# A decoder trunk in split fp32: when ScalarE copies the running sum of the feed-forward into its PSUM banks

## The chip, the cores and the metric

The kernel runs on one core of one Trainium2 chip. The metric is the device time of one execution in microseconds (us). Each kernel is run several times; before the change the median of three runs is 2176.53 us (2175.78 to 2177.68). One further execution was recorded by the profiler: 2176.25 us in all, of which 2174.5 us lie between its first and its last instruction (its span).

Engines, as the profile names them: PE is TensorE's matmul, PEld its weight load, DVE is VectorE, ACT is ScalarE, POOL is GpSimd, SP is SyncE, which issues nearly all DMAs here. A q behind a name means the engine's sequencer.

## The reference

Two decoder layers over 256 tokens of width 2048, in float32: a gated linear attention layer, then a differential attention layer, each followed by a feed-forward (FFN). What the change touches is the FFN alone:

```
def swiglu(h, w_gate_up, w_down):
    gate, up = jnp.split(h @ w_gate_up, 2, axis=-1)
    return (jax.nn.silu(gate) * up) @ w_down

for i in range(DEPTH):                       # DEPTH = 2
    ...                                      # mixer, x = x + rmsnorm(mix)
    f = swiglu(rmsnorm(x, pre_ffn_g[i]), ffn_w_gate_up[i], ffn_w_down[i])
    x = x + rmsnorm(f, post_ffn_g[i])
```

The hidden width is 5632, so `gate` and `up` have 11 chunks of 512 columns each, and the output has 4 chunks of 512.

## The kernel before

**Split products.** A float32 matmul is made of three products of a faster format: each operand is split into a high part (ScalarE's cast, L306) and a low part (VectorE subtracts the high part from the value, L309), and TensorE adds up high times high, high times low and low times high (L419 to L421, or L559 to L561). Weights come in blocks of 128 x 1024 (256 rows of a chunk of 512 columns). Each block is loaded by SP into one of five `raw` buffers, cast, subtracted, and lies then in one of nine places of a ring (`hi`, `lo`) until TensorE has used it.

**The weight stream.** The order in which blocks are needed is written out by hand (`weight_stream`, L84). `take` (L387) hands out the next block and calls `pump` (L380), which writes down conversions ahead of need, up to nine blocks past the last one freed, and loads up to five blocks past the last one converted.

**Who sets the order.** The program is traced from top to bottom, and a planner then simulates the engines and writes the order of each engine's instructions: of those that are ready in its simulation the one traced earlier goes first (`urgent` puts a piece ahead). On the chip each engine goes through its own order, so an instruction that waits holds up those behind it. `issue_after(x)` (used by `past`, L760, and `behind`, L395) forces what is traced inside it to come behind `x` on `x`'s engine.

**Up steps (duos).** For chunk c, `gated_duo` (L1253) makes gate and up together by `duo_seeded` (L490). Eight blocks of each of the two chunks are worked through, s = 0 to 7; the ones in `fast` (0, 2, 3, 4, 5, 6, or 0, 2, 4, 6 for c = 1) are combined by sums of blocks (kinds a to d, four conversions, L343 to L359), the others are done plainly; of a plain s below 7 the second chunk's block is kept for the end. The duo uses PSUM banks 0, 1, 3, 4, 5, 7 of the pool `acc` (six banks) and 2 and 6 of the pool `tp` (two). Behind the last fast step stands `early` (L1267): ScalarE copies bank 0 out (L1270), and VectorE takes differences with banks 5, 6 and 4 (L1259), one of which is the start value of bank 7. After it come the kept blocks, block 7 of the first chunk (banks 1 and 3) and block 7 of the second (banks 2 and 7), with `late` (L1276) behind each finished bank: sums on VectorE and the Silu on ScalarE (L1281).

**Down runs.** `down_act` (L462) multiplies the hidden chunks of one group (`FF_GROUPS`, L39: pairs of chunks, chunk 8 alone) with the down weights and adds to output chunks, two banks each (one for each half of the tokens). Only the first group starts from nothing. For all others the running sum, which lies in SBUF (`f_ffn`), is first copied into the two banks by ScalarE (L472), and TensorE adds onto it; at the end the banks are copied back (L1335). Down runs and duos alternate (`ffn_steps`, L60). In each FFN nine down runs begin with such copies: eight directly behind a duo, the ninth behind another down run.

In the text d0 and d1 are the first and second block of a down run, and blocks 7 the last ones of a duo. The functions that the change touches:

Of the kernel before, what the change touches and what calls it, by code (L numbers as in the profile page):

```python
# [54 lines left out]
def ffn_pairs(c):  # L55

    return FAST_SECOND if c == 1 else FAST_FFN
# [139 lines left out]
class Trunk:  # L197
    def __init__(self, ctx, tc, t):
        self.ctx, self.tc, self.nc, self.t = ctx, tc, tc.nc, t

        def pool(name, **kw):
            return ctx.enter_context(tc.tile_pool(name=name, bufs=1, **kw))

        self.const = pool("const")
        self.big = pool("big")
        self.ring = pool("ring")
        self.hs = pool("hs")
        self.psum = pool("psum", space=bass.MemoryType.PSUM)
        self.dram = pool("dram", space=bass.MemoryType.DRAM)
        self.n = 0  # L210
        self.later = []
        self.stream = weight_stream()
        self.loads = load_list(self.stream)
        self.n_used = self.n_done = 0
        self.subs = {}
        self.split_off = None
        self.parts = {}
        self.raws = {}
        self.n_dma = self.n_conv = self.n_take = self.n_free = 0
        self.pool_lo = set()  # L220
        self.n_narrow = 0
        self.cap = 2
        self.ident = self.const.tile([P, P], F32, tag="ident", name="ident")
# [78 lines left out]
    def split(self, src, gp=False):  # L302
        nc = self.nc
        w = src.shape[-1]
        hi, lo = self.places(w)
        cast = nc.scalar.copy(hi, src)  # L306
        eng = nc.gpsimd if gp else nc.vector
        with self.past(self.split_off):
            rest = eng.tensor_tensor(out=lo, in0=src, in1=hi.bitcast(F32), op=ALU.subtract)  # L309
        if not gp:  # L310
            self.parts[self.n_conv] = cast.ins, rest.ins
        return hi, lo
# [66 lines left out]

    def pump(self):  # L380
        n = len(self.stream)
        while self.n_conv < min(n, self.n_free + NRING, self.n_take + self.cap):
            self.convert()
            while self.n_dma < min(len(self.loads), self.n_done + NRAW):
                self.load()
# [76 lines left out]
    def down_act(self, aT, w, s0, order, ns, evac, skew=0, base=None):  # L462

        ps, taken = {}, {}

        def run(u, b):
            c, s = order[u]
            if c not in ps:
                ps[c] = [self.acc(), self.acc()]
                if base:  # L470
                    for i in range(2):
                        self.nc.scalar.copy(ps[c][i], base(c, i))  # L472
            if not b:
                taken[u] = self.take(w, (c, s0 + s))
            self.mm_act(ps[c][b], aT, b, s, taken[u], ns, base is not None)
            if s == ns - 1:
                evac(c, b, ps[c][b])
            if b:
                self.free()
            self.tick()  # L480

        n = len(order) - skew
        for u in range(n):
            run(u, 0)
            run(u, 1)
        for b in range(2):
            for u in range(n, len(order)):
                run(u, b)

    def duo_seeded(self, aT, forms, fast, chunks, early, late):  # L490

        ps, held = {}, []
        (w1, n1), (w2, n2) = chunks

        def bank_of(bank):
            if bank not in ps:
                ps[bank] = self.tp().rearrange("p j t -> p (j t)") if bank in (2, 6) else self.acc()
                return True
            return False

        def add(bank, a, wp, j, last, onto=False):
            first = bank_of(bank)
            self.triple(ps[bank], a, wp, j, first and not onto, last, onto)

        def plain(bank, s, b, wp, last, onto=False):
            for j in range(2):
                add(bank, aT.tokens(2 * s + j, b), wp, j, last and j == 1, onto)
            if last:
                with self.behind(LATE_BEHIND):
                    late(bank, ps)  # L510
            self.tick()

        for s in range(7):
            k1, k2 = 2 * s, 2 * s + 1
            if s not in fast:
                wp = self.take(w1, (n1, s))
                for b, bank in enumerate((1, 3)):
                    plain(bank, s, b, wp, False)
                self.free()
                held.append(s)  # L520
                continue
            f, last = forms.pairs.index(s), s == fast[-1]
            plan = {
                "a": ((0, aT.tokens(k1, 0)), (1, aT.tokens(k2, 0))),
                "b": ((6, forms.fast(f, 2)), (2, forms.fast(f, 3))),
                "c": ((5, forms.fast(f, 1)), (3, aT.tokens(k2, 1))),
                "d": ((4, forms.fast(f, 0)),),
            }
            for kind, prods in plan.items():
                wp = self.take("duo", (*chunks, s), kind)  # L530
                for j, (bank, a) in enumerate(prods):
                    add(bank, a, wp, j, last and bank in (0, 4, 5, 6))
                self.free()
                if kind != "d":
                    self.tick()
            if last:
                bank_of(7)
                with self.behind(EARLY_BEHIND):
                    self.urgent(early)(ps)
        kept = [(s, self.take(w2, (n2, s))) for s in held]  # L540
        for s, wp in kept:
            plain(2, s, 0, wp, False)
        wp = self.take(w1, (n1, 7))
        for b, bank in enumerate((1, 3)):
            plain(bank, 7, b, wp, True)
        for s, wp2 in kept:
            plain(7, s, 1, wp2, False, True)
            self.free()
        self.free()
        wp = self.take(w2, (n2, 7))  # L550
        plain(2, 7, 0, wp, True)
        plain(7, 7, 1, wp, True, True)
        self.free()
# [696 lines left out]
        self.defer(5, lambda: next_gain(3))  # L1250
        self.chunk_act(aT, w, 3, 8, self.urgent(evac(3)), tail=SKEW)

    def gated_duo(self, hT, forms, w, c, rs, new_sg):  # L1253

        nc = self.nc
        made = []

        def op(out, in0, in1, how):
            nc.vector.tensor_tensor(out=out, in0=in0, in1=in1, op=how)  # L1259

        def gated(b, up):
            sg = made[0]
            nc.vector.scalar_tensor_tensor(
                out=sg[:, b, :], in0=up, scalar=rs[b], in1=sg[:, b, :], op0=ALU.mult, op1=ALU.mult
            )

        def early(ps):  # L1267
            made.extend((new_sg(), self.scratch()))
            sg, v = made
            nc.scalar.copy(sg[:, 0, :], ps[0])  # L1270
            op(v, ps[5], sg[:, 0, :], ALU.subtract)
            op(sg[:, 1, :], ps[6], v, ALU.subtract)
            op(ps[7], ps[4], sg[:, 1, :], ALU.subtract)
            op(v, ps[4], v, ALU.add)

        def late(bank, ps):  # L1276
            sg, v = made
            if bank in (1, 3):
                b = bank // 2
                op(sg[:, b, :], ps[bank], sg[:, b, :], ALU.add)  # L1280
                nc.scalar.activation(sg[:, b, :], sg[:, b, :], AF.Silu, scale=rs[b])  # L1281
            elif bank == 2:
                op(v, ps[bank], v, ALU.add)
                gated(0, v)
            else:
                gated(1, ps[bank])

        self.duo_seeded(hT, forms, ffn_pairs(c), ((w, c), (w, 11 + c)), early, late)
        return made[0]

    def ffn(self, fp, hT, rs, gi, wgu, wd, post, after, name, reload, side=None):
# [50 lines left out]
        def part(c, b):  # L1342
            return f[0][:, b, c * C : (c + 1) * C]

        f = []
        plan = ffn_steps()
        for n, (kind, which, *chunks) in enumerate(plan):
            if kind == "up":
                sg = self.gated_duo(hT, forms, wgu, which, rs, new_sg) if which else gated_first()
                follow = plan[n + 1]  # L1350
                wait = 4 if which else 1
                if follow[0] == "down" and which not in follow[1]:
                    wait = 2 * len(down_order(*follow[1:])) + 1
                self.defer(wait, lambda sg=sg, c=which: gate_T(sg, c))
                continue
# [17 lines left out]
                    with self.behind(DOWN_BEHIND):  # L1373
                        evac(grp, c, b, ps)

            base = None if which == first else part
            self.down_act(gTs[which], wd, 2 * which[0], down_order(which, chunks), 2 * len(which), done, skew, base)

    def values(self, vp, aT, rs, i, steps, every):
# [349 lines left out]
```

## Time and profile before

| | before |
|---|---|
| median of three runs | 2176.53 us |
| the profiled execution, whole | 2176.25 us |
| its span | 2174.5 us |
| TensorE busy (matmul) | 2153.9 us, 99% |
| VectorE busy | 1942.6 us, 89% |
| ScalarE busy | 1376.5 us, 63% |
| HBM, mean rate over the span | 202 GB/s |
| granted TensorE clock | 0.999 |

How to read what is quoted further down. A row of the timeline has the start in us from the span's beginning, the duration in us, engine, line, operation, the tiles written and read (out<-in), their shapes, how many instructions the row merges, and in brackets how long the engine sat idle before it and what ended that. A row of the waits has who waited for what, the total in us, how many times and the longest. Matmuls overlap: a new one starts every 0.23 us while each row shows 0.39, so a busy TensorE can still lose time between starts.

### The profile page before, as it was taken

Reading aid. Unit: us, or ns where it says so; the run is one execution under the profiler, and the core shown is the slowest. Engines: PE = TensorE matmul, PEld = TensorE weight load, DVE = VectorE, ACT = ScalarE, POOL = GpSimd, SP = SyncE. Lnnn points to the kernel's source line nnn. Section 1 sums busy time; section 2 is a strip of 40 time slices with the busy share of each in tenths; the row PEclk is TensorE's granted clock in tenths of the full one; section 3 lists DMA queues with packets and bytes.
Section 4 is the critical chain, followed back from the end, with each engine's and each line's share of the span. In section 5 each row is a group of like instructions: output and inputs, shape, how many; then the busy total and the mean of one; then the engine's idle time right before and its main releaser. Section 6 shows DMA issues by size and latency. Waiting matters only on the chain.

```text
span 2174.5 us, 28418 instructions
## 1 busy us (share of the span) xinstructions
PE 2153.9 (99%) x10044; PEld 1785.0 (82%) x10044; DVE 1942.6 (89%) x2666; ACT 1376.5 (63%) x1926; POOL 38.4 (2%) x66
## 2 busy tenths in 40 slices
PE   9999999999999999999999999999999999999998
PEld 7888788888888888888878888888888888888876
DVE  7989988999999999999798567889999999999996
ACT  8756655666666666666776455566656666666664
POOL 1000000000000000000000000000000000000000
PEclk9999999999999999999999999999999999999999
DMA  8545566566555666656767555465655556566664
GB/s 309 166 150 192 176 225 214 208 220 231 174 191 205 213 213 209 207 181 214 249 203 244 188 172 163 149 235 186 228 202 185 188 200 209 202 210 205 210 215 154
DMA packets 125043, 440.08 MB, mean 202 GB/s; under 512 B 14091, under 2 KB 16820, under 8 KB 123620
## 3 DMA queue, kind: packets, MB, share of 16 engines
q1 hardware_dynamic: 123724, 436.44, 59.3%
q10 hardware_dynamic: 1176, 1.84, 0.2%
q8 instruction: 78, 1.28, 0.2%
q14 instruction: 65, 0.53, 0.1%
HBM read 429.82 MB, written 9.97 MB: 202 GB/s over the span
## 4 chain that ended last, share of the span: by engine, by line
PE 88%; DVE 5%; DMA 3%; ACT 2%; issue 1%; SPq 0%; POOL 0%; ACTq 0%; DVEq 0%; POOLq 0%
PE acc L419 11%; PE acc L421 11%; PE acc L420 11%; PE acc L560 10%; PE acc L561 10%; PE acc L559 10%; PE acc L707 8%; PE acc L708 4%; PE tp L561 3%; PE tp L560 3%; PE tp L559 3%; DMA raw<-in_w_d_dram 2%; DVE lo L309 2%; ACT hi L306 2%; DVE raw L341 1%
## 5 line engine op out<-in xcount | busy, mean ns | idle before, releaser
L309 DVE TENSOR_TENSOR lo<-raw,hi 128x1024 fp32r<-128x1024 f32 x921 | 1098.4, 1218 | 131.3 <-ACT hi L306 125.8
L306 ACT CAST hi<-raw 128x1024 fp32r<-128x1024 f32 x923 | 946.9, 1051 | 376.5 <-PE acc L707 89.6
L419 PE MATMUL acc<-hi,f_ffn_gT 128*128 128x512 f32 x704 | 270.5, 392 | 6.1 <-ACT acc L472 6.0
L420 PE MATMUL acc<-lo,f_ffn_gT 128*128 128x512 f32 x704 | 272.6, 389 | 0.0
L421 PE MATMUL acc<-hi,f_ffn_gT 128*128 128x512 f32 x704 | 270.5, 389 | 0.0
L560 PE MATMUL acc<-lo,h_ffn 128*128 128x512 f32 x612 | 239.2, 391 | 0.1
L561 PE MATMUL acc<-hi,h_ffn 128*128 128x512 f32 x612 | 238.4, 390 | 0.0
L559 PE MATMUL acc<-hi,h_ffn 128*128 128x512 f32 x612 | 227.7, 389 | 0.0
L419 PEld LDWEIGHTS acc<-hi,f_ffn_gT 128*128 128x128 f32 x704 | 132.1, 188 | 38.6 <-ACT acc L472 11.1
L341 DVE TENSOR_TENSOR raw<-raw 128x512 f32<-128x512 f32 x232 | 159.2, 686 | 3.3
L421 PEld LDWEIGHTS acc<-hi,f_ffn_gT 128*128 128x128 f32 x704 | 132.2, 188 | 27.5
L420 PEld LDWEIGHTS acc<-lo,f_ffn_gT 128*128 128x128 f32 x704 | 132.2, 188 | 27.2
L560 PEld LDWEIGHTS acc<-lo,h_ffn 128*128 128x128 f32 x612 | 114.9, 188 | 26.2 <-DVE lo L309 1.0
L559 PEld LDWEIGHTS acc<-hi,h_ffn 128*128 128x128 f32 x612 | 114.9, 188 | 24.1
L561 PEld LDWEIGHTS acc<-hi,h_ffn 128*128 128x128 f32 x612 | 114.9, 188 | 23.1
L306 ACT CAST hi<-sum 128x512 fp32r<-128x512 f32 x72 | 44.8, 622 | 96.6 <-DVE sum L341 96.6
L306 ACT CAST f_ffn_rest<-sum 128x512 fp32r<-128x512 f32 x56 | 34.9, 623 | 95.6 <-DVE sum L341 95.6
L707 PE MATMUL acc<-h_q,hi 128*128 128x512 f32 x256 | 92.5, 401 | 0.0
L707 PE MATMUL acc<-h_kv,hi 128*128 128x512 f32 x256 | 90.7, 399 | 0.0
L707 PE MATMUL acc<-h_mix,hi 128*128 128x512 f32 x256 | 90.5, 398 | 0.0
L1335 ACT COPY f_ffn<-acc 128x512 f32<-128x512 f32 x80 | 46.7, 586 | 56.6 <-PE acc L421 56.1
L341 DVE TENSOR_TENSOR sum<-raw,raw 128x512 f32<-128x512 f32 x116 | 79.3, 683 | 0.1
(417 smaller groups left out, 4105.8 us busy)
## 6 DMA issues: line engine op xcount, KB each, us to landing
raw<-in_w_gu_dram SPq DMA_DIRECT2D x352, 512.0 KB, 4.4
raw<-in_w_d_dram SPq DMA_DIRECT2D x176, 512.0 KB, 4.5
raw<-in_gla_w_r_dram SPq DMA_DIRECT2D x32, 512.0 KB, 4.4
raw<-in_gla_w_v_dram SPq DMA_DIRECT2D x32, 512.0 KB, 4.0
raw<-in_gla_w_out_dram SPq DMA_DIRECT2D x32, 512.0 KB, 4.8
raw<-in_w_v_dram SPq DMA_DIRECT2D x32, 512.0 KB, 4.5
raw<-in_w_k_dram SPq DMA_DIRECT2D x32, 512.0 KB, 4.3
raw<-in_diff_w_q_dram SPq DMA_DIRECT2D x32, 512.0 KB, 3.5
```

The source lines that it names most:

```text
L306: cast = nc.scalar.copy(hi, src)
L309: rest = eng.tensor_tensor(out=lo, in0=src, in1=hi.bitcast(F32), op=ALU.subtract)
L341: return self.nc.vector.tensor_tensor(out=out, in0=in0, in1=in1, op=ALU.add)
L419: nc.tensor.matmul(ps, ah, rh, start=(kt == 0 and not onto), stop=False, skip_group_check=onto)
L420: nc.tensor.matmul(ps, ah, rl, start=False, stop=False, skip_group_check=onto)
L421: nc.tensor.matmul(ps, al, rh, start=False, stop=(kt == 2 * ns - 1), skip_group_check=onto)
L559: nc.tensor.matmul(ps, ah, wh, start=first, stop=False, skip_group_check=onto)
L560: nc.tensor.matmul(ps, ah, wl, start=False, stop=False, skip_group_check=onto)
L561: nc.tensor.matmul(ps, al, wh, start=False, stop=last, skip_group_check=onto)
L707: nc.tensor.matmul(ps, lh, aT.both(kt), start=(kt == 0), stop=False)
L708: nc.tensor.matmul(ps[:, SEQ:], ll, aT.hi(kt), start=False, stop=(kt == KT - 1))
L1335: nc.scalar.copy(fc, ps)
```

## The change

The copies into the first two banks of a down run that follows a duo are traced inside that duo instead of at the run's start: the first directly behind `early`, the second behind the sums of banks 1 and 3 (`ahead`). `self.led` holds the latest such copy until the down run begins; casts traced meanwhile are tied behind it on ScalarE. So that casts of down weights are not traced ahead of the first copy, `open_to` stops `pump` from the start of the last but one fast step until `early` is traced; the number of blocks it lets through is that of the rest of the duo (in the duo of chunk 1, which has further plain steps, two fewer). The limit holds in every duo; copies move only where the next step is a down run that adds to an existing sum. The copies of a run's second chunk, and both pairs of the run that follows another run, stay at the run.

```
@@ __init__
+        self.open_to = self.led = None
@@ split
-        cast = nc.scalar.copy(hi, src)
+        with self.past(self.led):
+            cast = nc.scalar.copy(hi, src)
@@ pump
-        while self.n_conv < min(n, self.n_free + NRING, self.n_take + self.cap):
+        while self.n_conv < min(n, self.n_free + NRING, self.n_take + self.cap, self.open_to or n):
@@ down_act, run
-                ps[c] = [self.acc(), self.acc()]
-                if base:
-                    for i in range(2):
-                        self.nc.scalar.copy(ps[c][i], base(c, i))
+                ps[c] = base(c) if base else [self.acc(), self.acc()]
+                self.led = None
@@ duo_seeded(self, aT, forms, fast, chunks, early, late, ahead)
+            if s == fast[-2]:
+                self.open_to = self.n_take + 8 + len(held) + 2
...
             if last:
                 bank_of(7)
                 with self.behind(EARLY_BEHIND):
                     self.urgent(early)(ps)
+                self.open_to = None
+                ahead(0)
...
         for b, bank in enumerate((1, 3)):
             plain(bank, 7, b, wp, True)
+        ahead(1)
@@ ffn
+        def seed(c, b):
+            ps = self.acc()
+            self.led = nc.scalar.copy(ps, part(c, b)).ins
+            return ps
+
         f = []
+        seeded = []
...
-                sg = self.gated_duo(hT, forms, wgu, which, rs, new_sg) if which else gated_first()
                 follow = plan[n + 1]
+
+                def ahead(b, follow=follow):
+                    self.led = None
+                    if follow[0] == "down" and f and follow[1] != first:
+                        seeded.append(seed(down_order(*follow[1:])[0][0], b))
+
+                sg = self.gated_duo(hT, forms, wgu, which, rs, new_sg, ahead) if which else gated_first()
+                self.led = None
...
-            base = None if which == first else part
+            base = None if which == first else lambda c: [seeded.pop(0) if seeded else seed(c, b) for b in range(2)]
```

More of the change, by code (lines that the diff above doesn't have):

```diff
@@ L488, in down_act, with duo_seeded @@
                 run(u, b)
-    def duo_seeded(self, aT, forms, fast, chunks, early, late):
+    def duo_seeded(self, aT, forms, fast, chunks, early, late, ahead):
         ps, held = {}, []
@@ L1251, in proj_out, with gated_duo @@
         self.chunk_act(aT, w, 3, 8, self.urgent(evac(3)), tail=SKEW)
-    def gated_duo(self, hT, forms, w, c, rs, new_sg):
+    def gated_duo(self, hT, forms, w, c, rs, new_sg, ahead):
         nc = self.nc
@@ L1286, in late @@
                 gated(1, ps[bank])
-        self.duo_seeded(hT, forms, ffn_pairs(c), ((w, c), (w, 11 + c)), early, late)
+        self.duo_seeded(hT, forms, ffn_pairs(c), ((w, c), (w, 11 + c)), early, late, ahead)
         return made[0]
```

## The prediction

> **What bounds the kernel now.** I read the page first, then who waits for whom, then three rows of the timeline around the start of one down run. The page gives the span and TensorE's share:
>
> ```profile
> span 2174.5 us, 28418 instructions
> PE   2153.9 (99%) x10044; PEld 1785.0 (82%) x10044; DVE 1942.6 (89%) x2666; ACT 1376.5 (63%) x1926; POOL 38.4 (2%) x66
> ```
>
> TensorE has work 99% of the time, so a change that takes no matmul away can win at most what TensorE still waits, about 20 us. Of the waits that the trace names, these two matter:
>
> ```profile
> PE acc L419 <- ACT acc L472: 6.0, 9, 1.4
> ...
> ACT hi L306 <- DMA raw<-in_w_d_dram: 60.0, 85, 3.0
> ```
>
> The first (waits of TensorE: us in total, times, longest) is the first product of a down run that waits for ScalarE's copy of the running sum. The second says that ScalarE stands before casts whose down weights have not landed. One start of a down run shows how the two belong together. ScalarE:
>
> ```profile
> 713.42 0.58 ACT L1270 COPY sg<-acc 128x512 f32<-128x512 f32 x1
> 713.90 2.00 ACT L306 CAST hi<-raw 128x1024 fp32r<-128x1024 f32 x2
> 716.27 1.05 ACT L306 CAST hi<-raw 128x1024 fp32r<-128x1024 f32 x1 [0.37 <-DMA raw<-in_w_d_dram]
> 718.39 1.06 ACT L306 CAST hi<-raw 128x1024 fp32r<-128x1024 f32 x1 [1.07 <-DMA raw<-in_w_d_dram]
> 719.35 1.10 ACT L472 COPY acc<-f_ffn 128x512 f32<-128x512 f32 x2
> ```
>
> The copy out of bank 0 (the duo's early step) comes first, then the casts of the duo's two last blocks (block 7 of either chunk), then the casts of the first two down blocks, d0 and d1, each behind a DMA, and only then the two copies, with no idle time ahead of them: they were ready and stood in ScalarE's order behind d1's cast, 1.07 us of which was a wait for data that the first product doesn't need. TensorE meanwhile:
>
> ```profile
> 717.21 0.40 PE L560 MATMUL acc<-lo,h_ffn 128*128 128x512 f32 x1
> ...
> 719.05 0.39 PE L560 MATMUL acc<-lo,h_ffn 128*128 128x512 f32 x1
> 719.28 0.39 PE L561 MATMUL acc<-hi,h_ffn 128*128 128x512 f32 x1
> 719.99 0.50 PE L419 MATMUL acc<-hi,f_ffn_gT 128*128 128x512 f32 x1 [0.33 <-ACT acc L472]
> 720.33 0.40 PE L560 MATMUL tp<-lo,h_ffn 128*128 128x512 f32 x1
> ...
> 721.71 0.39 PE L420 MATMUL acc<-lo,f_ffn_gT 128*128 128x512 f32 x1
> ```
>
> Matmuls follow each other every 0.23 us (719.05 to 719.28). The down run's first one, put ahead of the duo's last ones in TensorE's order, starts 0.71 after its predecessor: the wait costs 0.48, not 0.33, and the next spacing (0.34) 0.11 more. **Each listed wait costs its own length and 0.26 us.** The other eight:
>
> ```profile
> 844.96 0.50 PE L419 MATMUL acc<-hi,f_ffn_gT 128*128 128x512 f32 x1 [0.38 <-ACT acc L472]
> 908.68 0.50 PE L419 MATMUL acc<-hi,f_ffn_gT 128*128 128x512 f32 x1 [1.31 <-ACT acc L472]
> 1035.03 0.50 PE L419 MATMUL acc<-hi,f_ffn_gT 128*128 128x512 f32 x1 [1.44 <-ACT acc L472]
> 1677.66 0.50 PE L419 MATMUL acc<-hi,f_ffn_gT 128*128 128x512 f32 x1 [0.38 <-ACT acc L472]
> 1803.03 0.50 PE L419 MATMUL acc<-hi,f_ffn_gT 128*128 128x512 f32 x1 [0.45 <-ACT acc L472]
> 1928.32 0.50 PE L419 MATMUL acc<-hi,f_ffn_gT 128*128 128x512 f32 x1 [0.32 <-ACT acc L472]
> 2053.55 0.50 PE L419 MATMUL acc<-hi,f_ffn_gT 128*128 128x512 f32 x1 [0.29 <-ACT acc L472]
> 2117.68 0.50 PE L419 MATMUL acc<-hi,f_ffn_gT 128*128 128x512 f32 x1 [1.08 <-ACT acc L472]
> ```
>
> All nine stand where a down run follows a duo, which is where the change acts.
>
> **The change part by part.** It removes no instruction.
>
> ```profile
> L472 ACT COPY acc<-f_ffn x80: 572/580/596, 593.6 to 2146.6; 128x512 f32<-128x512 f32 x80
> ```
>
> Of these 80 copies it moves 32: sixteen down runs (eight in each FFN) follow a duo and are not of the first group, and each has two copies for its first chunk. No DMA and no matmul is added.
>
> *What goes.* With both copies ahead of d0's cast, the first product needs d0's high part alone, cast by 716.27 + 1.05 = 717.32, long before 719.28. In seven of the nine places the wait should go in whole. In the two at 1035.03 and 2117.68 it can't, for there it is d0's own cast that the DMA delays:
>
> ```profile
> 1033.44 1.04 ACT L306 CAST hi<-raw 128x1024 fp32r<-128x1024 f32 x1 [2.98 <-DMA raw<-in_w_d_dram]
> 1034.39 1.10 ACT L472 COPY acc<-f_ffn 128x512 f32<-128x512 f32 x2
> ...
> 2116.09 1.05 ACT L306 CAST hi<-raw 128x1024 fp32r<-128x1024 f32 x1 [2.33 <-DMA raw<-in_w_d_dram]
> 2117.05 1.10 ACT L472 COPY acc<-f_ffn 128x512 f32<-128x512 f32 x2
> ```
>
> The cast ends at 1034.48; the first copy there took 0.58 and ended at 1034.97, and the product started 0.06 later. Without the copy between them the product starts at 1034.54, which saves 0.49; likewise 0.48 at 2117. The sum: 6.0 - 1.44 - 1.08 = 3.48 for the seven, 7 x 0.26 = 1.82 for their restarts, 0.97 for the two: **6.3 us less.** Bounds: nothing (the waits only change their name) and all nine in whole, 6.0 + 9 x 0.26 = 8.3.
>
> [...]
>
> *What the moved copies hold up.* ScalarE spaces operations of this size by 0.52 (the two copies end 1.10 after the first starts). Placed behind the copy out of bank 0, they push the casts of both blocks 7 and of d0 back by 0.52 or 1.04. Behind those casts stands VectorE:
>
> ```profile
> 715.21 0.69 DVE L1259 TENSOR_TENSOR hs<-acc,sg 128x512 f32<-128x512 f32 x1 [0.24 <-PE acc L561]
> 715.82 1.21 DVE L309 TENSOR_TENSOR lo<-raw,hi 128x1024 fp32r<-128x1024 f32 x1
> 716.95 0.68 DVE L1259 TENSOR_TENSOR sg<-tp,hs 128x512 f32<-128x512 f32 x1
> 717.55 2.35 DVE L309 TENSOR_TENSOR lo<-raw,hi 128x1024 fp32r<-128x1024 f32 x2
> 719.82 0.69 DVE L1259 TENSOR_TENSOR acc<-acc,sg 128x512 f32<-128x512 f32 x1
> ```
>
> The first block 7 is cast by 714.95 and subtracted from 715.82 on, because VectorE is held until 715.21 by TensorE's bank: 0.87 of cover. One copy leaves 0.35. Two would make the subtraction 0.17 late, and it ends at 717.03 where the product (717.21) would start 0.06 after it: 0.12 more of cover, so 0.05 a place, 0.8 over sixteen, or with a restart each 16 x 0.31 = 5.0. I take nothing, since the second copy is traced behind the duo's sums of banks 1 and 3; 5.0 is the other bound. The second block 7 and d0 are subtracted from 717.55 on and have more cover.
>
> *The limit on conversions (open_to) and the tie.* They keep casts of down weights behind the first copy. In the trace those casts stand behind the bank-0 copy already, so nothing that runs is held back: none, with 0.52 for d0 hidden as above. SP's loads keep their order among themselves; no queue is passed. In the duo of chunk 1 the limit stops two blocks early, at the blocks 7, and there too they are cast behind the bank-0 copy today:
>
> ```profile
> 457.42 0.58 ACT L1270 COPY sg<-acc 128x512 f32<-128x512 f32 x1
> 458.33 1.05 ACT L306 CAST hi<-raw 128x1024 fp32r<-128x1024 f32 x1 [0.33 <-DMA raw<-in_w_gu_dram]
> ```
>
> Casts tied to the second copy begin some six blocks on, behind d0 and d1.
>
> *The order that the planner writes.* TensorE's order comes from a simulated schedule, and earlier copies can shift it. What that costs is not in the trace; the nearest price is that of the first rival below, 4.3 us lost, and as much won if chance goes the other way; I take none.
>
> **Does the saved time stay saved?** VectorE must keep up. Two stretches from one down start to the next:
>
> ```profile
> 845.00:908.00 63.00, 62.37 (x278) 51.34 (x278) 60.21 (x72) 39.89 (x48) 0.00 (x0) 1.00 0.61 201
> 908.00:971.00 63.00, 62.32 (x278) 51.38 (x278) 59.21 (x71) 41.01 (x51) 0.00 (x0) 1.00 0.58 198
> ```
>
> VectorE (the third busy time) idles 2.8 and 3.8 us in each, more than the 0.6 to 1.6 that a start gives back, and 715.21 shows it waiting for TensorE at the duo's end. So I expect TensorE's gain to reach the end. Profiled execution: 2176.25 (span 2174.5 and 1.75 around it, 0.28 below the median of 2176.53); 2176.25 - 6.3 = **2170.0**.
>
> **The rivals.**
>
> *The wait moves to d0's low part.* If the planner now puts d0's six products together ahead of the duo's last ones, the second needs the low part, which VectorE ends at 717.55 + 2.35 = 719.90, so it starts at 719.96. The first would start at 719.51, the second at 719.74: a wait of 0.22 and 0.26 of restart, at nine places 4.3 us. 2170.0 + 4.3 = 2174.3. For it: such an order has TensorE work that is ready by the simulation; against it: today's order has one such product and then five others (L420 at 721.71), 1.3 us of cover even when shifted.
>
> *The change doesn't do what it says.* The planner leaves the copies behind d1's cast, or they wait for their operands there: 2176.3. Against it: d0's cast is traced behind the first copy and tied to it.
>
> *ScalarE's order is blocked by a copy that has no bank yet*: slower. Place: between the bank-0 copy and the first block 7's cast. If the first copy gets bank 5 instead of bank 0, it waits for VectorE's difference (715.21 + 0.69 = 715.90) and runs 715.96 to 716.54; the cast follows from 716.48 to 717.53, the subtraction starts 1.71 late, and the product waits 1.71 - 0.12 = 1.59 and 0.26 of restart. Sixteen times 1.85 = 29.6: 2170.0 + 29.6 = 2199.6. It decides from a hold of 0.99 us (0.87 + 0.12) and has eaten the gain at 1.12, where 16 x (0.13 + 0.26) = 6.3. Against it: bank 0 is free from 714.00, 1.9 us before bank 5. [...]
>
> **How the numbers follow.** Forecast 0.58, with a range of its own from 2168 (all nine waits) to 2172. Low part 0.17; no effect 0.10; blocked order 0.15, seldom at all sixteen places. The predicted time is 2170.0. The range goes from 2167.5 to 2178.0: below are the 8.3 of the bound, above the first two rivals and a blocked order at a few places; what is left out is most of the last rival and a little below. Some 0.2% (4.4 us) is what a measurement of this kernel can tell from no change, so faster means under 2172.2: 0.59, nearly all of the forecast. Within 0.2% lie the low part and no effect: 0.27. Slower: 0.14.
>
> **What would show it.** Right: TensorE's wait for the running-sum copy falls from 6.0 us to about 1.6 or goes over to d0's cast at the two places with a late DMA; the copies stand directly behind the bank-0 copy or the casts of the blocks 7, ahead of the casts with down weights. The first rival shows as waits of L420 for VectorE's low part, the last as idle ScalarE ahead of a copy and TensorE waiting for the low part of block 7. Wrong altogether would be waits in places where no down run starts.

## The result and the profile after

The changed kernel takes 2166.40 us (median of six runs, 2166.05 to 2166.81) against 2177.11 us of the kernel before, run beside it (six runs, 2175.78 to 2179.02): ratio 0.9951, 95% interval 0.9938 to 0.9963. Forecast were 2170.0 and a range from 2167.5 to 2178.0. The sign is right, the gain is larger than the range allowed: 10.7 us between the medians and 10.1 between the two profiled executions, where 6.3 were expected.

The page of the changed kernel, with the span, the busy times and the engines' shares of the chain that ended last:

```profile
span 2164.4 us, 28414 instructions
...
PE 2150.1 (99%) x10044; PEld 1785.7 (83%) x10044; DVE 1943.1 (90%) x2666; ACT 1375.8 (64%) x1926; POOL 38.4 (2%) x66
...
PE 96%; DVE 2%; DMA 1%; ACT 1%; issue 1%; SPq 0%; POOL 0%; DVEq 0%; POOLq 0%; ACTq 0%
```

The same row of the chain of the kernel before:

```profile
PE 88%; DVE 5%; DMA 3%; ACT 2%; issue 1%; SPq 0%; POOL 0%; ACTq 0%; DVEq 0%; POOLq 0%
```

The work is the same; the chain runs through TensorE for 96% of the span instead of 88%, since fewer waits lead it over to DMAs, VectorE and ScalarE. The waits of the changed kernel (who waited for what; us in total, times, longest), TensorE's two longest and one of ScalarE:

```profile
PE acc L831 <- POOL ones L856: 1.1, 1, 1.1
PE acc L423 <- DVE h_kv L783: 1.0, 1, 1.0
...
ACT hi L308 <- DMA raw<-in_w_d_dram: 59.4, 82, 2.4
```

No row with the running-sum copy is left (6.0 us in nine waits before), not even the 1.6 us that the prediction left standing. ScalarE waits for down weights as long as before (59.4 us against 60.0): the data comes no sooner, it is TensorE that no longer notices.

The start of the down run that the prediction followed, in the timeline of the changed kernel: ScalarE, then VectorE, then TensorE (L1275 is the copy out of bank 0, L308 the casts, L1352 the running-sum copies, L421 the first product of a down block, L564 to L566 the duo's products).

```profile
713.09 0.58 ACT L1275 COPY sg<-acc 128x512 f32<-128x512 f32 x1
713.57 2.00 ACT L308 CAST hi<-raw 128x1024 fp32r<-128x1024 f32 x2
715.47 0.59 ACT L1352 COPY acc<-f_ffn 128x512 f32<-128x512 f32 x1
715.99 1.06 ACT L308 CAST hi<-raw 128x1024 fp32r<-128x1024 f32 x1
717.98 1.06 ACT L308 CAST hi<-raw 128x1024 fp32r<-128x1024 f32 x1 [0.94 <-DMA raw<-in_w_d_dram]
718.94 0.58 ACT L1352 COPY acc<-f_ffn 128x512 f32<-128x512 f32 x1
...
718.34 0.69 DVE L1264 TENSOR_TENSOR acc<-acc,sg 128x512 f32<-128x512 f32 x1
718.95 0.68 DVE L1264 TENSOR_TENSOR hs<-acc,hs 128x512 f32<-128x512 f32 x1
719.54 2.35 DVE L311 TENSOR_TENSOR lo<-raw,hi 128x1024 fp32r<-128x1024 f32 x2
...
719.16 0.39 PE L565 MATMUL tp<-lo,h_ffn 128*128 128x512 f32 x1
...
720.07 0.39 PE L566 MATMUL tp<-hi,h_ffn 128*128 128x512 f32 x1
720.29 0.39 PE L421 MATMUL acc<-hi,f_ffn_gT 128*128 128x512 f32 x1
720.52 0.39 PE L564 MATMUL acc<-hi,h_ffn 128*128 128x512 f32 x1
```

Three orders have changed, and in nearly all of the sixteen places in the same way. **ScalarE**: the first copy stands behind the casts of the blocks 7 and ahead of d0's cast. The second still stands behind d1's, 0.94 us of waiting for data included: it moved hardly at all. **VectorE**: the start value of bank 7 (718.34) and the sum behind it come ahead of d0's low part, where before two low parts came first. **TensorE**: in the kernel before, d0's first product followed directly on the duo's products in banks 1 and 3, ahead of five products of bank 2 (719.99 and 720.33 of the rows there). Now the five come first, then that one product, then the duo's twelve of bank 7, and only behind them the rest of d0. Nothing in the diff orders TensorE; the planner did that.

So two things happened at once, and either could be the gain: the first product's operands come sooner, or the product comes later.

### The profile page after: what moved, and what is told of

It is laid out like the page before. It is cut to its first block, busy times and chain, and to the rows that moved or that the text cites. A ratio compares the mean times of both kernels' runs of the same rounds, so it can differ in the third digit from the quotient of the medians.

```text
span 2164.4 us, 28414 instructions
## 1 busy us (share of the span) xinstructions
PE 2150.1 (99%) x10044; PEld 1785.7 (83%) x10044; DVE 1943.1 (90%) x2666; ACT 1375.8 (64%) x1926; POOL 38.4 (2%) x66
## 4 chain that ended last, share of the span: by engine, by line
PE 96%; DVE 2%; DMA 1%; ACT 1%; issue 1%; SPq 0%; POOL 0%; DVEq 0%; POOLq 0%; ACTq 0%
PE acc L565 12%; PE acc L566 12%; PE acc L564 12%; PE acc L423 11%; PE acc L421 11%; PE acc L422 11%; PE acc L712 8%; PE acc L713 4%; PE tp L564 4%; PE tp L565 4%; PE tp L566 4%; PE tp L733 1%; DMA raw<-in_w_gu_dram 1%; DVE lo L311 1%; PE acc L1464 0%
## 5 line engine op out<-in xcount | busy, mean ns | idle before, releaser
L308 ACT CAST hi<-raw 128x1024 fp32r<-128x1024 f32 x923 | 947.4, 1051 | 392.1 <-DVE raw L343 92.4
L421 PE MATMUL acc<-hi,f_ffn_gT 128*128 128x512 f32 x704 | 269.3, 391 | 0.0
L566 PE MATMUL acc<-hi,h_ffn 128*128 128x512 f32 x612 | 238.3, 390 | 0.0
L564 PE MATMUL acc<-hi,h_ffn 128*128 128x512 f32 x612 | 227.7, 389 | 0.0
L421 PEld LDWEIGHTS acc<-hi,f_ffn_gT 128*128 128x128 f32 x704 | 132.2, 188 | 27.7 <-DVE sg L1268 0.6
L564 PEld LDWEIGHTS acc<-hi,h_ffn 128*128 128x128 f32 x612 | 114.9, 188 | 24.1
L566 PEld LDWEIGHTS acc<-hi,h_ffn 128*128 128x128 f32 x612 | 114.9, 188 | 23.3
L308 ACT CAST hi<-sum 128x512 fp32r<-128x512 f32 x72 | 44.8, 622 | 82.1 <-DVE sum L343 82.1
L308 ACT CAST f_ffn_rest<-sum 128x512 fp32r<-128x512 f32 x56 | 34.9, 623 | 94.7 <-DVE sum L343 94.7
L343 DVE TENSOR_TENSOR raw<-sum,raw 128x512 f32<-128x512 f32 x116 | 79.4, 684 | 0.0
```

The lines of the kernel that those rows point to most:

```text
L343: return self.nc.vector.tensor_tensor(out=out, in0=in0, in1=in1, op=ALU.add)
L421: nc.tensor.matmul(ps, ah, rh, start=(kt == 0 and not onto), stop=False, skip_group_check=onto)
L564: nc.tensor.matmul(ps, ah, wh, start=first, stop=False, skip_group_check=onto)
L566: nc.tensor.matmul(ps, al, wh, start=False, stop=last, skip_group_check=onto)
```

## The experiments

The theory after the result: the gain is TensorE's new order, and the early copy matters through the planner alone. The rival is the prediction's own: the gain is the copy that no longer stands behind d1's cast. Ten further kernels were run; every time below is a median beside the kernel before on the same chip (2177.11 to 2177.56 us), with the ratio and its 95% interval. The third column gives the order of TensorE's products from the end of banks 1 and 3 on: five of the duo's in bank 2, twelve of the duo's in bank 7, and those of the down run.

| kernel | copies | TensorE at the start of a down run | us | ratio |
|---|---|---|---|---|
| changed kernel | first early | five, d0's first, twelve, d0 | 2166.40 | 0.9951 (0.9938 to 0.9963) |
| pe_order | late | five, fourteen of the down run, twelve | 2168.65 | 0.9961 (0.9946 to 0.9976) |
| orders | late | five, twelve, d0 | 2166.37 | 0.9953 (0.9939 to 0.9967) |
| pe_order2 | late | five, twelve, d0; VectorE later at bank 7 | 2181.54 | 1.0018 (1.0009 to 1.0027) |
| order_only | late | d0's first, five, one more of the down run, twelve; VectorE as the changed kernel | 2178.04 | 1.0004 (0.9994 to 1.0013) |
| old_order | first early | d0's first, five, twelve | 2172.12 | 0.9977 (0.9968 to 0.9986) |
| no_tie | late | as before | 2176.53 | 0.9998 (0.9989 to 1.0008) |
| first_only | first early | as the changed kernel | 2166.88 | 0.9950 (0.9935 to 0.9965) |
| both_early | both early | five, twelve, d0 | 2166.42 | 0.9947 (0.9932 to 0.9962) |
| both_first | both ahead of the blocks 7 | six of bank 7 ahead of all these, later two of the down run, five, six | 2181.38 | 1.0017 (1.0008 to 1.0027) |
| two_places | in the last duo of each FFN alone | there as the changed kernel | 2175.20 | 0.9992 (0.9982 to 1.0001) |

**pe_order: TensorE's order without any copy moved.** The kernel before, its first down product tied behind the duo's last product of bank 2:

```
@@ duo_seeded
         plain(2, 7, 0, wp, True)
+        self.tail = self.last_mm.ins
         plain(7, 7, 1, wp, True, True)
@@ down_act, run
-            self.mm_act(ps[c][b], aT, b, s, taken[u], ns, base is not None)
+            with self.past(self.tail):
+                self.mm_act(ps[c][b], aT, b, s, taken[u], ns, base is not None)
+            self.tail = None
```

(`last_mm` is the product written down last.)

> The kernel before with one edit: TensorE's first product of a down run comes behind the duo's last product into bank 2, which is five products (5 x 0.2275 = 1.14 us) later than before. ScalarE's copies stay where they were, behind the cast of d1, and VectorE's order stays. Theory 'order': the copies' lateness is hidden by the duo's own last products. Of the waits of before (first spacing too long by 0.49, 0.54, 1.47, 0.16, 1.60, 0.54, 0.61, 0.26, 0.49, 0.45 and 1.25 us, and 0.11 in the next) only those above 1.14 leave something: 0.33, 0.46 and 0.11, with 0.11 each behind them. Saved: 9.1 - 1.2 = 7.9 us, a span of 2166.6 and a time near 2168.6. Theory 'copies' (the prediction's): it is their place on ScalarE that costs, and they have not moved: span 2174.5, time near 2176.7; TensorE waits for the copies as before.

2168.65 us against 2177.31: 8.7 us (by the interval 5.2 to 11.8) of the change's 10.7, and ScalarE and VectorE go through the same orders as before. The place followed above, ScalarE and TensorE (L420 is the first product of a down block):

```profile
719.21 1.09 ACT L473 COPY acc<-f_ffn 128x512 f32<-128x512 f32 x2
...
719.06 0.39 PE L565 MATMUL acc<-hi,h_ffn 128*128 128x512 f32 x1
...
720.42 0.62 PE L420 MATMUL acc<-hi,f_ffn_gT 128*128 128x512 f32 x2
```

The copies begin at 719.21, as late as ever. In the old order the first product would have been due at 719.29; it now comes at 720.42, with no idle time ahead. With five products of 0.23 us ahead of the first one, TensorE's list of waits has no row with the copy left, where the kernel before has 6.0 us in nine.

**orders and pe_order2: the changed kernel's orders with the copies late.** In orders the copies are made at the start of the run, as in the kernel before, and ties give TensorE (d0's products behind the duo's last one) and VectorE (low parts of down blocks behind the start value of bank 7) the changed kernel's orders, but for d0's first product, which stands behind the twelve like the rest of d0:

```
@@ ffn, ahead
-                    if follow[0] == "down" and f and follow[1] != first:
+                    if False:
@@ split
-        with self.past(self.split_off):
+        with self.past(self.split_off), self.past(self.led_v):
@@ early
-            op(v, ps[4], v, ALU.add)
+            self.led_v = self.add(v, ps[4], v).ins
@@ duo_seeded
         plain(7, 7, 1, wp, True, True)
+        self.tail = self.last_mm.ins
@@ down_act, run
+            with self.past(self.tail):
                 self.mm_act(ps[c][b], aT, b, s, taken[u], ns, base is not None)
```

> The changed kernel with its two copies put back to the start of the down run, behind the casts of d0 and d1, while TensorE's and VectorE's orders are kept as the change made them, by two ties (d0's products behind the duo's last bank-7 product; the low parts of the down blocks behind the start value of bank 7). The theory that the gain is the order of TensorE says: 17 products of 0.23 us = 3.9 us stand between the duo's listed products and d0's first one, more than the longest wait of before (1.44), so no wait for the copies is left and the time is the changed kernel's, 2166.4 (2165.5 to 2167.5). If copies that stand late still cost something, as the prediction's sum has it, up to 6.3 us of the gain are missing: 2168 to 2172.7.

2166.37 us, the changed kernel's time. The timeline of orders, ScalarE and TensorE:

```profile
718.75 1.05 ACT L308 CAST hi<-raw 128x1024 fp32r<-128x1024 f32 x1 [1.53 <-DMA raw<-in_w_d_dram]
719.70 1.10 ACT L1354 COPY acc<-f_ffn 128x512 f32<-128x512 f32 x2
...
723.10 0.39 PE L568 MATMUL acc<-hi,h_ffn 128*128 128x512 f32 x1
723.33 0.39 PE L421 MATMUL acc<-hi,f_ffn_gT 128*128 128x512 f32 x1
```

The copies stand where they stood before, behind d1's cast with 1.53 us of waiting, and end at 720.80. In the old order the first product would have been due near 719.5. Here it comes at 723.33, with 2.5 us to spare. With the two other engines' orders given, it is worth nothing that the copies are early.

pe_order2 has the tie on TensorE alone, on the kernel before. The planner answers it on VectorE: a sum more, and at seven places a low part more, stands ahead of bank 7's start value than before.

> The kernel before, with all products of the down run tied on TensorE behind the duo's last bank-7 product, and nothing else. If TensorE's order alone is enough: 2166.4, as the changed kernel. If bank 7 needs VectorE's new order as well: here VectorE makes the start value of bank 7 behind one or two more operations than before (a sum of 0.69 us, at half the places also a low part of 1.2 us), it ends about 721.1 to 722.3 on the clock of the start at 719, and the bank-7 products that would follow at 720.6 wait 0.5 to 1.7 us and 0.26 of restart at 16 places: 2178 to 2190, slower than before.

2181.54 us, slower than before. The row of its waits and one place in its timeline, VectorE and TensorE:

```profile
PE acc L562 <- DVE acc L1262: 13.4, 15, 1.5
```

```profile
913.68 0.68 DVE L1262 TENSOR_TENSOR sg<-acc,sg 128x512 f32<-128x512 f32 x1
914.28 1.21 DVE L310 TENSOR_TENSOR lo<-raw,hi 128x1024 fp32r<-128x1024 f32 x1
915.41 0.69 DVE L1262 TENSOR_TENSOR acc<-acc,sg 128x512 f32<-128x512 f32 x1
...
914.24 0.39 PE L564 MATMUL tp<-hi,h_ffn 128*128 128x512 f32 x1
916.15 0.50 PE L562 MATMUL acc<-hi,h_ffn 128*128 128x512 f32 x1 [1.53 <-DVE acc L1262]
```

TensorE now comes to bank 7 directly behind the five products of bank 2, but VectorE makes low parts and a sum first and reaches bank 7's start value at 915.41. The two orders belong together: this kernel is 15 us slower than orders, which has both. What TensorE's new order costs beside VectorE's old one is not shown, since VectorE's got worse with the tie.

**order_only: VectorE's order, without TensorE's.** As orders, without the tie on TensorE. The planner leaves d0's first product where it was, ahead of the five, but puts the duo's twelve ahead of most of the down run here too.

> The limit stays, the copies go back to the start of the run, and instead the low parts of the down blocks are tied on VectorE behind the early step's last sum. The planner then gives VectorE the changed kernel's order, leaves the copies behind the cast of d1 and TensorE's first down product where it was, ahead of the duo's last products. Theory 'order on TensorE or copies on ScalarE': neither has moved, so the waits for the copies stay: span 2173 to 2175, time near 2176.5. Rival: it is VectorE's earlier start value for bank 7 that matters: 2167 to 2170.

2178.04 us: nothing won. The waits of TensorE:

```profile
PE acc L421 <- ACT acc L1352: 7.9, 14, 1.4
```

**old_order: the early copy in TensorE's old order.** The changed kernel, with d0 taken early and the first product of d0 put ahead of the block 7's products of bank 2, which are tied behind it (the code that leaves this product out of the down run later is not shown):

```
@@ duo_seeded
-        plain(2, 7, 0, wp, True)
+        with self.past(ahead(2)):
+            plain(2, 7, 0, wp, True)
@@ ffn, ahead
                     if follow[0] == "down" and f and follow[1] != first:
+                        if b == 2:
+                            c, s = down_order(*follow[1:])[0]
+                            self.pre = self.take(wd, (c, 2 * follow[1][0] + s))
+                            ah = gTs[follow[1]].hi(2 * s, slice(0, P))
+                            return nc.tensor.matmul(seeded[0], ah, self.pre[0][:, :C], start=False, stop=False, skip_group_check=True).ins
```

> The changed kernel, but TensorE's first product of a down run is forced back ahead of the duo's last block (its six bank-2 products come behind it). Copies, tie and limit stay. Prediction's sum: fourteen places lose their waits, the two with a late DMA still wait for d0's own cast; against the changed kernel that is 1.1 and 0.8 us of waiting and 0.26 of restart for each, 2.4 us in all: span 2166.8, time near 2168.8, TensorE waiting for ScalarE's cast at two places. Theory 'order alone': what the change saves comes from TensorE's order, so that most of it is gone again: 2174 or more.

2172.12 us, between the two expectations. Its waits for the start of a down run, and the later of the two places in the timeline:

```profile
PE acc L1374 <- ACT hi L308: 2.4, 2, 1.8
```

```profile
2113.52 1.04 ACT L308 CAST hi<-raw 128x1024 fp32r<-128x1024 f32 x1 [1.79 <-DMA raw<-in_w_d_dram]
...
2112.46 0.39 PE L570 MATMUL acc<-hi,h_ffn 128*128 128x512 f32 x1
2114.62 0.50 PE L1374 MATMUL acc<-hi,f_ffn_gT 128*128 128x512 f32 x1 [1.76 <-ACT hi L308]
```

This is the prediction's mechanism laid bare. Fourteen places have no wait for the copy, with the product where it was. At the two places with a late DMA the wait remains and has changed its name to d0's cast, as the prediction had it. So the early copy does free the first product. It wins 5.2 us against the kernel before, and 5.9 against order_only, which has the same order on VectorE, nearly the same on TensorE, and the copies late.

What is missing to the prediction's 2168.8 lies elsewhere. The edit ties all six products of block 7 in bank 2, where only five stood behind d0's first one before. So one product fewer stands ahead of the first that needs the low part of the first block 7: at fifteen places it is the tenth behind the product that VectorE's first difference waits for, not the eleventh. The prediction gave the eleventh 0.12 us of cover, so the tenth comes 0.2275 - 0.12 = 0.11 us late, and the next spacing has 0.11 more, as behind the listed waits: an estimate of 15 x 0.22 = 3.3 us, and 2168.8 + 3.3 is 2172.1. In the profiled execution the granted clock was lower as well (0.997, last section); seven of the ten executions have a granted clock of 0.999, as nearly all of the other kernels' have, so the median holds little of that.

TensorE's order is worth 8.7 by itself (pe_order), and where the changed kernel's orders are in place, early copies find nothing left to win (orders).

**no_tie: what writes the order.** The changed kernel without the tie of the casts behind the copies:

```
@@ split
-        with self.past(self.led):
-            cast = nc.scalar.copy(hi, src)
+        cast = nc.scalar.copy(hi, src)
```

> The changed kernel without the tie: copies are traced in the duo and conversions are held until the early step, but casts may go ahead of the copies. The planner then writes the three engines' orders around each duo as in the kernel before (copies behind the cast of d1). Theory 'order' and the planner: as before, span 2174.5, time near 2176.7, TensorE waiting 6 us for the copies. Theory 'earlier tracing is enough': 2166.4, as the changed kernel.

2176.53 us, the orders of all engines around these places are those of the kernel before, and so are the waits:

```profile
PE acc L420 <- ACT acc L1351: 5.6, 8, 1.1
```

Tracing the copy early is not enough: the planner puts d0's and d1's casts ahead of it again. The tie makes d0's cast later in its simulation, and (this is argued from the orders, not shown) a d0 that is ready later no longer goes ahead of the duo's own products.

**first_only, both_early, both_first: which copy, and how early.** In first_only the second call of `ahead` does nothing; in both_early the first call makes both copies; in both_first the limit is two blocks lower besides, so that the casts of the blocks 7 come behind the copies:

```
@@ both_first, duo_seeded
-                self.open_to = self.n_take + 8 + len(held) + 2
+                self.open_to = self.n_take + 8 + len(held)
@@ both_early and both_first, ahead
-                    if follow[0] == "down" and f and follow[1] != first:
-                        seeded.append(seed(down_order(*follow[1:])[0][0], b))
+                    if not b and follow[0] == "down" and f and follow[1] != first:
+                        for i in range(2):
+                            seeded.append(seed(down_order(*follow[1:])[0][0], i))
```

> Only the first bank's copy is made in the duo; the second one stays at the start of the down run. Theory 'order': TensorE's and VectorE's orders are as in the changed kernel, and the second copy comes at the same place of ScalarE's order: 2166.4, span 2164.4. Rival: the second bank's copy, now queued behind casts that wait for DMA, brings back a wait at the down run's second bank, up to the 6.0 us of before: 2167 to 2172.

> The changed kernel with both copies traced directly behind the early step; the planner puts both between the casts of the blocks 7 and d0's, and d0's first product behind all of the duo. Theory 'order': nothing is left to win at these places and nothing is held up: within 0.5 us of the changed kernel, span 2164 to 2165, time near 2166.4. Rival: the second copy's slot in front of d0's cast delays d0's low part (0.52 a place, with a restart 0.3 to 0.8 at sixteen places): 5 to 12 us slower than the changed kernel.

> Both copies directly behind the copy out of bank 0, ahead of the casts of the blocks 7 (the limit stops two blocks earlier and these casts are tied too). The prediction's bound: block 7's low part is 0.17 us late beyond its cover, 0.8 us over sixteen places without and 5.0 with a restart at each: 2167.2 to 2171.4. Theory 'order': the planner knows of the hold and lets VectorE seed bank 7 first and TensorE use it first, so nothing is lost: 2166.4 plus or minus 0.5.

2166.88, 2166.42 and 2181.38 us. The first two are the changed kernel's time within what can be measured: the second copy's place is worth nothing, and more than one early copy isn't needed. both_first is 15.0 us slower than both_early, which neither expectation had. Its waits, and one place: ScalarE, VectorE, TensorE.

```profile
PE acc L564 <- DVE acc L1264: 11.6, 16, 0.7
```

```profile
717.68 0.59 ACT L1352 COPY acc<-f_ffn 128x512 f32<-128x512 f32 x1 [1.17 <-DVE hs L1264]
718.21 3.90 ACT L308 CAST hi<-raw 128x1024 fp32r<-128x1024 f32 x4
...
718.40 0.70 DVE L1264 TENSOR_TENSOR acc<-acc,sg 128x512 f32<-128x512 f32 x1
...
718.04 0.39 PE L566 MATMUL tp<-hi,h_ffn 128*128 128x512 f32 x1
719.16 0.50 PE L564 MATMUL acc<-hi,h_ffn 128*128 128x512 f32 x1 [0.73 <-DVE acc L1264]
```

The second copy has no bank until VectorE's difference has read it, and ScalarE idles 1.17 us ahead of it with the casts of the blocks 7 behind: the place and the kind of hold that the prediction's last rival named. What TensorE pays is another thing: its order now puts bank 7 so early that it waits for the start value, 1.12 - 0.23 = 0.89 us and 0.11 in the next spacing, at all sixteen places. That makes 16.0 us against 15.0 measured.

**two_places: the change in the last duo of each FFN alone.** These hold the two places with a late DMA (1035 and 2117 in the kernel before).

```
@@ duo_seeded
-            if s == fast[-2]:
+            if s == fast[-2] and n1 == 10:
@@ ffn, ahead
-                    if follow[0] == "down" and f and follow[1] != first:
+                    if follow[0] == "down" and follow[1] == last:
```

> The change at two of its sixteen places only: the last duo of each FFN, where the first down block's DMA is late. The prediction's sum gives 0.97 us there (the cast of d0 stays in the way): span 2173.5, time near 2175.7. Theory 'order': the whole of both waits goes, 1.60 + 1.25 + 2 x 0.11 = 3.1 us: span 2171.4, time near 2173.6.

2175.20 us; the interval of the ratio (0.9982 to 1.0001, so 0 to 4 us) holds both expectations. Inconclusive as to size. In its trace both places have no wait, and the others together have more than they had in the trace of the kernel before: nine waits for the copy, 5.1 us, where the seven other listed places had 3.48. Each of the nine listed waits of before stands behind a cast that waited 1.06 to 2.98 us for its DMA, and such a wait is not the same in every trace: d1's cast at the place followed above waited 1.07 us in the kernel before, 0.94 in the changed kernel and 1.53 in orders.

## Why the prediction was right and wrong

**Right: what bound the kernel, and that the gain would stay.** What TensorE's start-to-start times have above 0.2275 us, summed over all its 10044 products, falls from 42.9 to 32.8 us. The span falls by the same 10.1. VectorE did not become the bound (2% of the chain after, 5% before).

**Right: 0.26 us of restart behind each listed wait.** The sum needs it: the nine listed waits with their restarts are 6.0 + 9 x 0.26 = 8.3 us, and none of them is left.

**Wrong: the two places with a late DMA.** The failed step is "In the two at 1035.03 and 2117.68 it can't, for there it is d0's own cast that the DMA delays", together with "The order that the planner writes ... I take none". The step took TensorE's order as fixed. The changed kernel at the first of these places, ScalarE and TensorE:

```profile
1029.55 1.05 ACT L308 CAST hi<-raw 128x1024 fp32r<-128x1024 f32 x1 [2.21 <-DMA raw<-in_w_d_dram]
...
1029.77 0.39 PE L565 MATMUL tp<-lo,h_ffn 128*128 128x512 f32 x1
...
1030.68 0.39 PE L566 MATMUL tp<-hi,h_ffn 128*128 128x512 f32 x1
1030.91 0.39 PE L421 MATMUL acc<-hi,f_ffn_gT 128*128 128x512 f32 x1
```

d0's cast ends at 1030.60, late as in the kernel before. In the old order the product would have been due at 1029.77 and have waited 0.89; five products of the duo have come between, and it starts at 1030.91 with no idle time. The two places thus gave 1.44 + 1.08 + 2 x 0.26 = 3.04 us, where the sum had 0.97. old_order is the check: with the old order of these products, the two waits are back.

**Wrong: the bound of 8.3 us.** It counted the waits that the trace lists, and took them for all there are. (Nor are the 20 us without a busy TensorE a bound: rows of 0.39 us with a start every 0.23 overlap, so a lost start can leave TensorE busy; the 42.9 us above are what the starts had lost.) Four more starts were late before, each by less than the lists show. Two of them, in the timeline of TensorE before:

```profile
970.76 0.39 PE L561 MATMUL acc<-hi,h_ffn 128*128 128x512 f32 x1
971.15 0.50 PE L419 MATMUL acc<-hi,f_ffn_gT 128*128 128x512 f32 x1
971.49 0.39 PE L560 MATMUL tp<-lo,h_ffn 128*128 128x512 f32 x1
...
1737.39 0.39 PE L559 MATMUL tp<-hi,h_ffn 128*128 128x512 f32 x1
1737.85 0.50 PE L560 MATMUL acc<-lo,h_ffn 128*128 128x512 f32 x1
1738.19 0.40 PE L561 MATMUL acc<-hi,h_ffn 128*128 128x512 f32 x1
```

No bracket stands behind them, but 971.15 comes 0.39 behind its predecessor and the next one 0.34 behind it, 0.27 us in all; its twin at 1865.56 lost 0.36. The one at 1737.85 is a block 7's product that waits for its low part and loses 0.23 + 0.11; there is one like it at 1988.54. In these rows a duration of 0.50 instead of 0.39 marks such a start. Together 1.3 us, and none is left in the changed kernel. At the last two TensorE's own order made the difference: the late product was the ninth behind the one that VectorE's first difference waits for, where at the other fourteen places it was the eleventh. It is still the ninth, and late, in pe_order; in the changed kernel and in order_only it is the eleventh there too, and on time.

The gain of 10.1 us is then 6.3 as predicted, 2.1 at the two late places, 1.3 at the four unlisted starts; the remaining 0.4 was not traced to a place.

**Right in kind, but not what decided: the seven waits.** The prediction said that the first product would need d0's high part alone, so that the waits go. old_order shows that this holds. But in the changed kernel it was not put to use: orders has the late copies and the same time, within what can be measured.

**"What the moved copies hold up: nothing"** held for the change (block 7's first low part starts 0.61 us after the start of VectorE's difference, before and after). The upper bound of that term did not hold: for both copies ahead of the blocks 7 the prediction gave 0.8 or 5.0 us, and both_first lost 15.0, since the orders of VectorE and TensorE turned with it.

**The rivals.** The wait for d0's low part did not come, since all of d0 but one product stands behind the duo's end. "The change doesn't do what it says" describes no_tie, so the tie, costed at nothing, is what makes the change work at all. That a copy lacks a bank does not fit the changed kernel: its first copy runs at 715.47 with no idle time of ScalarE ahead of it, so a bank was free for it almost 5 us before the product at 720.29.

## What to carry to other kernels

Where a planner writes the engines' orders, an edit on one engine is also an edit of the others' orders: look first at what the late instruction stands ahead of, and try to move it behind that, before moving its operands forward. Such a change needs the order of the engine that feeds the pulled-up work too (pe_order2, where that engine came later instead, is 15 us slower than orders). And a bound on the gain from waits is made from start-to-start times, not from listed waits alone.

## What the runs showed of the hardware

In the trace of old_order the granted clock is halved twice while TensorE has work, each time for 3.41 us. The stretch ahead of each and the halved one (from:to, length, busy us and number of PE, PEld, DVE, ACT and POOL, then the granted clock, the DMA share and GB/s):

```profile
1088.53:1091.94 3.41, 1.70 (x7) 0.86 (x5) 3.41 (x9) 3.38 (x12) 0.06 (x1) 1.00 0.66 265
1091.94:1095.36 3.42, 3.37 (x10) 2.88 (x11) 3.42 (x7) 2.85 (x9) 0.49 (x1) 0.50 0.89 275
2112.53:2115.94 3.41, 1.65 (x8) 1.11 (x7) 2.40 (x3) 2.42 (x3) 0.00 (x0) 1.00 1.01 404
2115.94:2119.36 3.42, 3.42 (x10) 2.65 (x9) 3.29 (x4) 3.35 (x5) 0.00 (x0) 0.50 0.76 217
```

At half the clock a product starts every 0.43 us instead of 0.23 (2117.10 to 2117.52). The later halving stands behind the wait of 1.76 us at 2114.62, the earlier one behind two of 1.03 and 0.73 us (at 1089.82 and 1091.99). The kernel before has the same two, 1.03 and 0.74 us (at 1092.42 and 1094.59). Two stretches of it, the first around the first wait alone, the second around both:

```profile
1090.26:1093.67 3.41, 2.38 (x12) 1.49 (x10) 3.41 (x8) 3.38 (x10) 0.00 (x0) 1.00 0.64 258
1091.30:1094.71 3.41, 1.64 (x7) 0.98 (x7) 3.41 (x10) 3.38 (x12) 0.24 (x1) 1.00 0.65 261
```

There the clock stays at 1.00 behind both waits too, though the second stretch has 1.64 us of TensorE's work and the two ahead of the halvings have 1.70 and 1.65. So the work in 3.41 us does not by itself tell whether a halving follows. The two halvings begin 1024.00 us apart, 300 times 3.413, and last about that long (3.41 and 3.42). In the kernel before the clock's last change, to 0.50 at 2168.87, is 315 such steps behind 1093.67, which lies between the two waits. That the clock changes at such steps alone, and that the waits of the kernel before fell into two of them, is the author's estimate from these three changes; the traces do not settle it.

The profiled execution of old_order was the longest of its ten (2175.0 us, 2.9 over the median). Two stretches of 3.41 us at half the clock cost 3.4 us at most, by an estimate of 2 x 3.41 / 2.
